# A hybrid S5/Hyena encoder layer in fp32: the input projections in another order

## Chip, core and metric

The kernel runs on one core of one Trainium2 chip. The metric is device time in microseconds (us); less is better. All data are fp32 in DRAM; the large products run in fp32r with a split into a high and a low part (three products per product).

## What is computed

One layer of a bidirectional encoder with x of 1024 tokens by 1024 channels:

```
xn = rmsnorm(x);  proj = xn @ w_in                      # 1024 x 7168
u_s5, g_s5, p_hy, g_hy, m_logits = split(proj)          # 512, 512, 3072, 1024, 2048
y_s5 = s5_mixer(u_s5, g_s5, ...) @ w_branch_s5          # scan both ways, GELU, GLU, * silu(g_s5)
v, x1, x2 = split(short_conv_3(p_hy))                   # centred, width 3
z = v
for o, g in enumerate((x1, x2)):                        # two long convolutions by FFT
    z = g * (irfft(rfft(z, 2L) * kf[o])[:L] + d[o] * z)
y_hy = (z * silu(g_hy)) @ w_branch_hy
m = sigmoid(m_logits)
out = rmsnorm(x + (m[:, :1024] * y_s5 + m[:, 1024:] * y_hy) @ w_out)
```

## The kernel before

**Projections.** A projection makes one block of 128 output channels for all 1024 tokens (`proj`, L528; `projs`, L532): 3 passes (high weight by high x, high by low x, low by high x) of 16 matmuls of 128x512 into a PSUM tile `pps` of which there are two, then a function `use` that empties it. The 56 column blocks of `w_in` are named by number here: 0 to 3 are u, 4 to 7 the S5 gate, 8 to 15 v, 16 to 23 x1, 24 to 31 x2, 32 to 39 the Hyena gate (SiLU), 40 to 55 the merge gates m (sigmoid). The products with `s5_w_glu` and `w_branch_s5` have half as many matmuls (24). Weights come through a short pipeline (`prefetch`, L501): a load on SP's queue into one of three `wraw` buffers, a cast on ScalarE (`whi`), a subtraction mostly on GpSimd (`wlo`), two buffers each. The list `self.order` (L492) gives the order of the weights, so the order of the projections is fixed.

**Emptying.** A gate block (`merge_gate`, L729) needs one ScalarE activation and a store to DRAM. A v, x1 or x2 block needs `conv` (L555): one ScalarE pass and two VectorE passes (L564, L566), then a fold of the time axis on VectorE and GpSimd (L782 and L783 for v, L585 to L587 for x1, L589 to L591 for x2). All of these pass through the two buffers `cv` of the pool `ev`.

**Stages.** After the filters come: the S5 scan, four blocks of channels (`s5_block`), bound up with VectorE's scans, with three merge gates beside each block; two v blocks and the last four merge gates; the S5 tail (`s5_tail`, L1259: reload the scan's result `d_y` as `ty`, split it into `tyh` and `tyl`, GLU products, one more v block, the branch products); the forward spectra of v (`hy_forward0`, L789: transposes `zt` of the folded v, DFT matmuls `fwe` and `fwo`, products with the filter spectra on VectorE, store to DRAM) with the other v blocks as they are needed; the first way back (`hy_inverse0`, L806: inverse DFT matmuls `iv`, times x1, transposed again); the second spectra (`hy_forward1`, L846), beside pairs of Hyena gate and x2 blocks; the second way back (`hy_inverse1`), branch product, merge, output product.

**Who sets the order.** A scheduler reorders the instructions of the program before it is compiled, by priorities and estimated times; on the chip each engine then runs its own list strictly in order, and waits at the head of it. Matmuls of projections are put among the DFT matmuls by that scheduler.

Of the kernel before, what the change touches and what calls it, by code (L numbers as in the profile page):

```python
# [9 lines left out]
F = mybir.dt.float32  # L10
# [7 lines left out]
L = 1024  # L18
# [82 lines left out]
class Trunk:  # L101
# [627 lines left out]
    def merge_gate(self):  # L729

        nc, c = self.nc, self.n_m
        if c == 16:
            return
        self.n_m += 1

        def use_m(ps):
            t = self.ev.tile([128, L], F, name="cv")
            nc.scalar.activation(out=t, in_=ps, func=AF.Sigmoid)
            nc.scalar.dma_start(out=self.d_m[c], in_=t)
        self.proj(40 + c, use_m)  # L740
# [31 lines left out]
    def hy_v(self):  # L772

        nc, c = self.nc, self.n_v
        if c == 8:
            return
        self.n_v += 1

        def use_v(ps):
            t = self.conv(ps, c, "cv")  # L780
            o = self.folded[c] = self.vp.tile([128, 2, 2, 2, 128], F, name="fv")
            nc.vector.tensor_tensor(out=o[:, 0], in0=self.plus(t), in1=self.minus(t), op=ALU.add)  # L782
            nc.gpsimd.tensor_tensor(out=o[:, 1], in0=self.plus(t), in1=self.minus(t), op=ALU.subtract)  # L783
            nc.vector.tensor_copy(out=o[:, 0, 0, 0, 0:1], in_=t[:, 512:513])
            nc.vector.tensor_scalar(out=o[:, 1, 0, 0, 0:1], in0=t[:, 0:1], scalar1=-1.0, scalar2=None, op0=ALU.mult)

        self.proj(8 + c, use_v)

    def hy_forward0(self):  # L789

        with ExitStack() as ctx:
            wp, fwd = self.fwd_pools(ctx, 0)
            for c in range(10):
                while self.n_v < min(8, c + 1):
                    self.hy_v()
                if c % 2 and c > 1:
                    next(f), next(f)
                if 0 < c < 9:
                    if c % 2:
                        z = wp.tile([128, 2, 2, 8, 128], R, name="z")  # L800
                    self.to_time(self.pf, self.folded.pop(c - 1).rearrange("p a b c d -> p (a b c d)"), z[:, (c - 1) % 2])
                if c % 2 == 0 and c:
                    f = fwd(c // 2 - 1, z)
                    next(f), next(f)

    def hy_inverse0(self):  # L806
# [3 lines left out]
        with ExitStack() as ctx:  # L810
# [3 lines left out]
            pt = ctx.enter_context(tc.tile_pool(name="iv_pt", bufs=2, space=PSUM, side="right"))  # L814
            gates, back = {}, {}
# [17 lines left out]
            for c in range(10):  # L833
# [7 lines left out]
                if 0 < c < 9:  # L841
                    rotate(c - 1)
                if c > 1:
                    store(c - 2)

    def hy_forward1(self, tail):  # L846

        nc = self.nc
        self.d_x2 = self.dram.tile([8, 128, L], F, name="d_x2")
        with self.tc.tile_pool(name="sg", bufs=1) as sp, self.tc.tile_pool(name="vf1", bufs=2) as self.vf, \  # L850
# [14 lines left out]
            for c in range(8):  # L865
                silu = sp.tile([128, L], F, name="sg")

                def use_g(ps):
                    nc.scalar.activation(out=silu, in_=ps, func=AF.Silu)

                def use_x2(ps):
                    t = self.vf.tile([128, 2, 2, 2, 128], F, name="vf")
                    self.fold(self.conv(ps, 16 + c, "cv"), silu, t)
                    nc.scalar.dma_start(out=self.d_x2[c], in_=t.rearrange("p a b c d -> p (a b c d)"))

                for i, (col, use) in enumerate(((32 + c, use_g), (24 + c, use_x2))):
                    self.proj(col, use)
                    for _ in range((2, 3, 0)[(2 * c + i) % 3]):
                        next(f, None)
                    if 2 * c + i == 11:  # L880
                        ctx.close()
                        tail()
# [191 lines left out]
    def s5_first(self, gb, p4, sp, ps_s):  # L1074
# [7 lines left out]
        self.merge_gate()  # L1082
# [33 lines left out]
    def s5_block(self, gb, p4, sp, ps_s):  # L1116
# [32 lines left out]
        self.merge_gate()  # L1149
# [77 lines left out]
        self.merge_gate()  # L1227
# [15 lines left out]
    def s5_inputs(self, c0, c1):  # L1243
        nc, d = self.nc, self.dram
        if c0 == 0:
# [4 lines left out]
            self.n_m = 0  # L1250
# [163 lines left out]
    def run(self):  # L1414
        tc = self.tc
        with ExitStack() as ctx:
# [28 lines left out]
            with ExitStack() as c4:  # L1445
                with tc.tile_pool(name="fv", bufs=3) as self.vp:
                    self.d_spec, self.folded, self.n_v = {}, {}, 0
                    with tc.tile_pool(name="vf0", bufs=2) as self.vf:
                        self.hy_v()
                        self.hy_v()  # L1450
                        while self.n_m < 16:
                            self.merge_gate()
                        self.s5_tail()
# [30 lines left out]
```

## Time and profile before

| | us |
|---|---|
| median of 3 runs | 1487.98 (1487.80 to 1488.49) |
| the profiled execution | 1488.18 |
| its span, first to last instruction | 1486.4 |
| TensorE busy in the span | 1358.1 (91%) |
| VectorE busy | 1100.0 (74%) |
| ScalarE, GpSimd busy | 447.0, 486.4 |

The profiled execution lies 0.2 us above the median, and 1.8 us of it lie outside the span. TensorE is busy nine tenths of the time, and the amount of its work does not depend on the order; so the table is read for where TensorE is not busy, and which engine it waits for there.

### The profile page before, as it was taken

Reading aid. Unit: us, or ns where it says so; the run is one execution under the profiler, and the core shown is the slowest. Engines: PE = TensorE matmul, PEld = TensorE weight load, DVE = VectorE, ACT = ScalarE, POOL = GpSimd, SP = SyncE. Lnnn points to the kernel's source line nnn. Section 1 sums busy time; section 2 is a strip of 40 time slices with the busy share of each in tenths; the row PEclk is TensorE's granted clock in tenths of the full one; section 3 lists DMA queues with packets and bytes.
Section 4 is the critical chain, followed back from the end, with each engine's and each line's share of the span. In section 5 each row is a group of like instructions: output and inputs, shape, how many; then the busy total and the mean of one; then the engine's idle time right before and its main releaser. Section 6 shows DMA issues by size and latency. Waiting matters only on the chain. (4 is left out here: it accounts for less than half of the span.)

```text
span 1486.4 us, 19375 instructions
## 1 busy us (share of the span) xinstructions
PE 1358.1 (91%) x7219; PEld 1143.8 (77%) x7219; DVE 1100.0 (74%) x1963; ACT 447.0 (30%) x661; POOL 486.4 (33%) x306
## 2 busy tenths in 40 slices
PE   5888999998988989899999998999999944999998
PEld 3767888786867868688888776888888844978886
DVE  7999996899789887525479998454569994943532
ACT  4666662122222122232121211333321112511322
POOL 3756764114111111234223312245412111333222
PEclk9998999999999999899999999999999976999999
DMA  8221224622652323243853345645477669633432
GB/s 270 86 71 72 106 86 158 170 86 71 216 160 77 86 74 74 78 143 116 276 182 114 128 140 188 191 158 167 156 267 265 219 209 314 205 131 112 127 111 75
DMA packets 177673, 220.52 MB, mean 148 GB/s; under 512 B 21853, under 2 KB 142937, under 8 KB 174844
## 3 DMA queue, kind: packets, MB, share of 16 engines
q1 hardware_dynamic: 149212, 153.69, 33.8%
q10 hardware_dynamic: 27792, 62.45, 11.6%
q0 software_dynamic: 576, 3.15, 0.6%
q8 instruction: 57, 0.93, 0.3%
q14 instruction: 36, 0.29, 0.1%
HBM read 147.49 MB, written 76.82 MB: 151 GB/s over the span
## 5 line engine op out<-in xcount | busy, mean ns | idle before, releaser
L513 POOL TENSOR_TENSOR wlo<-wraw,whi 128x1024 fp32r<-128x1024 f32 (+1 forms) x67 | 169.6, 2533 | 588.1 <-PE pps L542 412.4
L542 PE MATMUL pps<-xh,whi 128*128 128x512 f32 x896 | 234.4, 408 | 11.5 <-DVE cv L566 11.5
L542 PE MATMUL pps<-xh,wlo 128*128 128x512 f32 x896 | 228.1, 401 | 0.0
L542 PE MATMUL pps<-xl,whi 128*128 128x512 f32 x896 | 226.0, 399 | 0.0
L542 PEld LDWEIGHTS pps<-xh,whi 128*128 128x128 f32 x896 | 169.9, 194 | 50.1 <-issue 12.3
L542 PEld LDWEIGHTS pps<-xh,wlo 128*128 128x128 f32 x896 | 169.2, 191 | 38.9
L542 PEld LDWEIGHTS pps<-xl,whi 128*128 128x128 f32 x896 | 167.9, 190 | 38.9 <-issue 0.2
L510 ACT CAST whi<-wraw 128x1024 fp32r<-128x1024 f32 (+1 forms) x76 | 74.7, 984 | 348.3 <-PE pps L542 276.1
L404 PE MATMUL po<-sh,fo 128*128 128x256 f32 x512 | 101.4, 292 | 6.0 <-DVE sh L111 5.1
L635 PEld LDWEIGHTS iv<-ic,y 128*128 128x128 f32 x752 | 96.5, 193 | 4.8 <-DVE y L113 2.3
L113 DVE TENSOR_TENSOR y<-yraw,y 128x512 fp32r<-128x512 f32 x64 | 61.7, 979 | 51.5 <-ACT y L109 51.2
L635 PE MATMUL iv<-ic,y 128*128 128x256 f32 (+1 forms) x752 | 98.4, 286 | 1.5 <-DVE y L113 1.5
L404 PEld LDWEIGHTS po<-sh,fo 128*128 128x128 f32 x512 | 84.3, 197 | 8.2 <-DVE sh L111 6.1
L357 POOL TENSOR_TENSOR acc<-acc,sq 128x512 f32<-128x512 f32 x56 | 76.3, 1362 | 25.0 <-ACT sq L342 22.8
L404 PE MATMUL po<-sl,fo 128*128 128x256 f32 x256 | 74.4, 291 | 1.0 <-DVE sl L113 1.0
L109 ACT CAST y<-yraw 128x512 fp32r<-128x512 f32 x64 | 39.3, 620 | 92.3 <-PE iv L635 54.1
L722 DVE TENSOR_TENSOR m<-m 128x512 f32<-128x512 f32 x64 | 53.0, 848 | 0.0
L404 PEld LDWEIGHTS po<-sl,fo 128*128 128x128 f32 x256 | 50.5, 197 | 2.3 <-DVE sl L113 1.5
L686 PE MATMUL fwo<-z,zc 128*128 128x256 f32 x384 | 50.1, 283 | 0.5 <-DVE x L716 0.5
L333 PE MATMUL g<-w3h,ha 128*128 128x512 f32 x64 | 33.0, 516 | 19.1 <-DVE e L338 17.3
L686 PEld LDWEIGHTS fwo<-z,zc 128*128 128x128 f32 x384 | 48.5, 191 | 1.6 <-DVE x L716 0.7
L336 ACT ACTIVATE e<-dec,negt 128x512 f32<-128x512 f32 x64 | 45.2, 716 | 10.6 <-DVE so L350 4.8
(437 smaller groups left out, 2685.1 us busy)
## 6 DMA issues: line engine op xcount, KB each, us to landing
wraw<-w_in SPq DMA_DIRECT2D x56, 512.0 KB, 4.6
kspec<-ko SPq DMA_DIRECT2D x32, 512.0 KB, 3.0
kt<-kspec SPq DMA_DIRECT2D x32, 512.0 KB, 3.3
d_y<-x ACTq DMA_DIRECT2D x32, 512.0 KB, 6.0
yraw<-d_y SPq DMA_DIRECT2D x64, 256.0 KB, 4.8
d_m<-cv ACTq DMA_DIRECT2D x16, 512.0 KB, 2.9
d_z<-z ACTq DMA_DIRECT2D x8, 1024.0 KB, 9.8
z<-d_z SPq DMA_DIRECT2D x8, 1024.0 KB, 10.9
```

The source lines that it names most:

```text
L109: nc.scalar.copy(out=hi, in_=src)
L113: e.tensor_tensor(out=lo, in0=src, in1=hi, op=ALU.subtract)
L333: nc.tensor.matmul(out=ps, lhsT=ha[:, tsl], rhs=w3h, start=True, stop=False)
L336: nc.scalar.activation(out=e, in_=decf, func=AF.Exp, scale=negt[:, tt:tt + 1])
L357: nc.gpsimd.tensor_tensor(out=acc, in0=acc, in1=sq, op=ALU.add)
L404: nc.tensor.matmul(out=po[:, part], lhsT=fo[a][:, 12 * (jj % 2) + b], rhs=sd[4 + i][d][:, part], start=n == 0 and part == 0, stop=n == 11 ...
L510: nc.scalar.copy(out=hi, in_=raw)
L513: eng.tensor_tensor(out=lo, in0=raw, in1=hi, op=ALU.subtract)
L542: nc.tensor.matmul(out=ps[:, hf * 512:hf * 512 + 512], lhsT=w[:, kc], rhs=part(x, kc, hf), start=a == 0 and p == 0 and kc == 0, stop=b == ...
L635: nc.tensor.matmul(out=dst, lhsT=lhsT, rhs=self.ic[b][:, j, cols], start=first, stop=last)
L686: nc.tensor.matmul(out=out, lhsT=zc[a][:, b], rhs=z[:, :, d, zi], start=start and n == 0, stop=stop and n == 3 * len(prods) - 1)
L722: nc.vector.tensor_tensor(out=m[:, part, :, 0], in0=m[:, part, :, 0], in1=m[:, part, :, 1], op=op)
```

## The change

The gate blocks (merge and Hyena gate, 24 "pure" blocks, ScalarE alone) become one list and can stand anywhere; the Hyena gates go to DRAM (`d_sg`) and are loaded again when their x2 block is folded. The S5 blocks take twelve pure blocks as before. The four merge gates that stood behind the scan are gone from there. All eight v blocks are made in and right behind the S5 tail, stored to DRAM (`d_v`) and loaded again for the transposes. Six pure blocks stand beside the forward spectra. The first way back has its eight x1 blocks and four x2 blocks, the second spectra six pure blocks and the other four x2 blocks, of which the last two are written behind the spectra.

```
-        self.order = i(range(0, 8), range(40, 52), range(8, 10), range(52, 56))
+        self.pure = [*range(40, 48), *range(32, 40), *range(48, 56)]
+        self.order = i(range(0, 8), self.pure[:12], range(8, 10))
         self.order += [("s5_w_glu", c, 4) for c in range(4)] + i(range(10, 11))
-        self.order += [("w_branch_s5", c, 4) for c in range(8)] + i(range(11, 24))
-        self.order += i(*((32 + c, 24 + c) for c in range(8)))
+        self.order += [("w_branch_s5", c, 4) for c in range(8)] + i(range(11, 16), self.pure[12:18])
+        self.order += i(*((16 + c,) + ((24 + c // 2,) if c % 2 else ()) for c in range(8)))
+        self.order += i(self.pure[18:20], (28,), self.pure[20:22], (29,), self.pure[22:24], (30, 31))
...
+    def gate_columns(self):
+        nc, col = self.nc, self.pure.pop(0)
+        func, out = (AF.Sigmoid, self.d_m[col - 40]) if col >= 40 else (AF.Silu, self.d_sg[col - 32])
+        def use(ps):
+            t = self.ev.tile([128, L], F, name="cv")
+            nc.scalar.activation(out=t, in_=ps, func=func)
+            nc.scalar.dma_start(out=out, in_=t)
+        self.proj(col, use)
+
+    def hy_x2(self, c, sp, vp):
+        nc = self.nc
+        def use_x2(ps):
+            silu = sp.tile([128, L], F, name="sg")
+            nc.sync.dma_start(out=silu, in_=self.d_sg[c])
+            t = vp.tile([128, 2, 2, 2, 128], F, name="vf")
+            self.fold(self.conv(ps, 16 + c, "cv"), silu, t)
+            nc.scalar.dma_start(out=self.d_x2[c], in_=t.rearrange("p a b c d -> p (a b c d)"))
+        self.proj(24 + c, use_x2)
...
         def use_v(ps):
             t = self.conv(ps, c, "cv")
-            o = self.folded[c] = self.vp.tile([128, 2, 2, 2, 128], F, name="fv")
+            o = self.vp.tile([128, 2, 2, 2, 128], F, name="fv")
...
+            nc.scalar.dma_start(out=self.d_v[c], in_=o.rearrange("p a b c d -> p (a b c d)"))
...
             for c in range(10):
-                while self.n_v < min(8, c + 1):
+                while self.n_v < 8:
                     self.hy_v()
+                if c < 8:
+                    folded[c] = self.vp.tile([128, L], F, name="fv")
+                    self.nc.sync.dma_start(out=folded[c], in_=self.d_v[c])
+                if c > 1 and len(self.pure) > 6:
+                    self.gate_columns()
...
                 if 0 < c < 9:
                     rotate(c - 1)
+                if c < 8 and c % 2:
+                    self.hy_x2(c // 2, sp, sp)
...
-            for c in range(8):
...
-                for i, (col, use) in enumerate(((32 + c, use_g), (24 + c, use_x2))):
-                    self.proj(col, use)
-                    for _ in range((2, 3, 0)[(2 * c + i) % 3]):
+            for i in range(10):
+                if i == 8:
+                    for _ in f:
+                        pass
+                    ctx.close()
+                    tail()
+                if i < 8 and i % 3 < 2:
+                    self.gate_columns()
+                else:
+                    self.hy_x2((4, 5, 6, 7)[i // 3 if i < 8 else i - 6], sp, self.vf)
+                if i < 8:
+                    for _ in range(2 if i % 2 else 3):
                         next(f, None)
...
                         self.hy_v()
                         self.hy_v()
-                        while self.n_m < 16:
-                            self.merge_gate()
                         self.s5_tail()
```

How the engines' lists change, at three places. TensorE at the end of the S5 scan (`s5ps` are the last products of the scan, `sr` and `si` its VectorE results; `pps` with `xh`, `xl` is a projection from x, with `tyh`, `tyl` one from the scan's reloaded result). Before:

```order
1365 L542 MATMUL pps<-xl,whi 128x512 x16
1366 L542 MATMUL pps<-xh,wlo 128x512 x16
1367 L542 MATMUL pps<-xh,whi 128x512 x16
1368 L542 MATMUL pps<-xl,whi 128x512 x5
1369 L1236 MATMUL s5ps<-sr,pr 128x128 x2
1370 L542 MATMUL pps<-xl,whi 128x512 x11
```

Between row 1390, the last product of the scan, and row 1401, the first with `tyh`, the list before holds the rest of this projection and three more from x. Now:

```order
1365 L544 MATMUL pps<-xl,whi 128x512 x16
1366 L544 MATMUL pps<-xh,wlo 128x512 x16
1367 L1253 MATMUL s5ps<-sr,pr 128x128 x2
1368 L1254 MATMUL s5ps<-si,pi 128x128
```

and the scan's last product is followed at once by the products with the reloaded result:

```order
1386 L1254 MATMUL s5ps<-si,pi 128x128
1387 L544 MATMUL pps<-tyh,whi 128x512 x14
1388 L544 MATMUL pps<-tyl,whi 128x512 x6
1389 L544 MATMUL pps<-tyh,whi 128x512 x2
1390 L544 MATMUL pps<-tyl,whi 128x512 x8
1391 L544 MATMUL pps<-tyh,wlo 128x512 x8
```

ScalarE's list at the same place (`y` is the GELU of the scan's products, `d_v` the new store of a folded v, `d_g` the S5 gate, `ty` the reload). Now:

```order
321 L1255 ACT_TABLE_LOAD
322 L1255 ACTIVATE y<-s5ps 128x512 x2
323 L798 DMA d_v<-fv 128x1024
324 L1294 DMA cv<-d_g 128x1024
325 L798 DMA d_v<-fv 128x1024
326 L1294 DMA cv<-d_g 128x1024
327 L1285 DMA ty<-d_y 128x1024 x4
328 L1286 CAST tyh<-ty 128x1024 x4
```

Before, one sigmoid, its table load and its store stood between `y` and the reload; now two stores of v and two gate loads do.

VectorE's list where the second spectra begin (`ke` is their first product; L564 and L566, now L566 and L568, are the two passes of `conv`, L590 and L591, now L592 and L593, the fold of an x2 block). Before:

```order
1480 L564 SCALAR_TENSOR_TENSOR cv<-pps,cw,cv 128x1023
1482 L566 SCALAR_TENSOR_TENSOR cv<-pps,cw,cv 128x1023
1484 L590 TENSOR_TENSOR vf<-cv,sg 128x512
1485 L591 TENSOR_TENSOR vf<-cv,sg 128x1
1486 L513 TENSOR_TENSOR wlo<-wraw,whi 128x1024
1487 L704 TENSOR_TENSOR ke<-fwe,eo_9003 128x512
```

Now:

```order
1487 L515 TENSOR_TENSOR wlo<-wraw,whi 128x1024
1488 L566 SCALAR_TENSOR_TENSOR cv<-pps,cw,cv 128x1023
1489 L568 SCALAR_TENSOR_TENSOR cv<-pps,cw,cv 128x1023
1490 L592 TENSOR_TENSOR vf<-cv,sg 128x512
1491 L593 TENSOR_TENSOR vf<-cv,sg 128x1
1492 L706 TENSOR_TENSOR ke<-fwe,eo_9414 128x512
```

The block folded here is the fourth x2 block before and the fifth now; from `ke` to the end of the spectra the list held four more before (rows 1487 to 1640) and holds three now (rows 1492 to 1640). On TensorE the number of projection matmuls ahead of the first DFT matmul of the second spectra, over the whole program, is 11 higher than before.

## Rows read from the trace of the kernel before

**Rows 1.** The page: span, and TensorE's line of part 1.

```profile
span 1486.4 us, 19375 instructions
PE 1358.1 (91%) x7219; PEld 1143.8 (77%) x7219; DVE 1100.0 (74%) x1963; ACT 447.0 (30%) x661; POOL 486.4 (33%) x306
```

**Rows 2.** Waits of TensorE: us in total, times, longest.

```profile
PE iv L633 <- DMA yraw<-d_y: 40.3, 1, 40.3
PE s5ps L1236 <- DVE sr L1223: 17.1, 3, 6.6
PE pps L542 <- DVE cv L566: 11.5, 2, 7.2
```

**Rows 3.** Windows by stage: us, busy PE, PEld, DVE, ACT, POOL, clock, DMA, GB/s.

```profile
735.00:746.00 11.00, 11.00 (x49) 8.86 (x48) 5.11 (x6) 3.18 (x6) 2.43 (x1) 1.00 1.02 364
746.00:884.00 138.00, 133.92 (x740) 113.94 (x739) 130.62 (x165) 29.11 (x36) 37.63 (x13) 0.99 0.39 132
884.00:936.80 52.80, 48.43 (x202) 38.63 (x201) 42.59 (x48) 10.17 (x10) 10.21 (x4) 0.97 0.63 209
936.80:1092.00 155.20, 155.20 (x885) 134.66 (x884) 79.52 (x125) 51.90 (x74) 66.65 (x35) 1.00 0.54 176
1092.00:1207.30 115.30, 115.08 (x647) 99.70 (x645) 106.13 (x136) 19.44 (x22) 15.83 (x6) 1.00 0.68 232
1207.30:1247.80 40.50, 0.23 (x2) 0.02 (x1) 26.87 (x31) 2.87 (x3) 8.83 (x2) 0.53 0.81 273
```

**Rows 4.** Timeline of TensorE, end of the scan: start, us, what, idle before.

```profile
591.95 3.90 PE L542 MATMUL pps<-xh,wlo 128*128 128x512 f32 x16
603.01 6.62 PE L542 MATMUL pps<-xh,whi 128*128 128x512 f32 x16 [7.17 <-DVE cv L566]
...
613.88 0.38 PE L1237 MATMUL s5ps<-si,pi 128*128 128x128 f32 x2
...
618.26 3.76 PE L542 MATMUL pps<-xh,wlo 128*128 128x512 f32 x15
...
651.72 3.90 PE L542 MATMUL pps<-xh,wlo 128*128 128x512 f32 x16
655.46 2.02 PE L542 MATMUL pps<-tyh,whi 128*128 128x512 f32 x8
```

**Rows 5.** Timeline of VectorE at the same place.

```profile
606.37 1.22 DVE L1226 TENSOR_TENSOR si<-si,f 128x1024 f32<-128x1024 f32 x1
...
618.10 4.11 DVE L782 TENSOR_TENSOR fv<-cv 128x512 f32<-128x512 f32 x2 [9.32 <-PE s5ps L1235]
...
635.37 3.82 DVE L1269 TENSOR_TENSOR tyl<-ty,tyh 128x1024 fp32r<-128x1024 f32 x2 [0.67 <-ACT tyh L1268]
```

**Rows 6.** Timeline of ScalarE at the same place.

```profile
618.54 0.60 ACT L1238 ACTIVATE y<-s5ps 128x512 f32<-128x512 f32 x1 [1.64 <-PE s5ps L1237]
...
625.50 2.09 ACTq L1267 DMA_DIRECT2D ty<-d_y  x4
631.07 1.05 ACT L1268 CAST tyh<-ty 128x1024 fp32r<-128x1024 f32 x1 [6.20 <-DMA ty<-d_y]
...
636.16 1.03 ACT L1268 CAST tyh<-ty 128x1024 fp32r<-128x1024 f32 x1
```

**Rows 7.** Timeline of GpSimd at the same place.

```profile
618.14 6.08 POOL L783 TENSOR_TENSOR fv<-cv 128x512 f32<-128x512 f32 x2 [19.82 <-PE s5ps L1235]
```

**Rows 8.** Timeline of TensorE behind the first spectra.

```profile
901.84 5.52 PE L542 MATMUL pps<-xh,whi 128*128 128x512 f32 x16 [4.37 <-DVE cv L566]
```

**Rows 9.** VectorE by line, 950 to 1250 us: busy, mean ns.

```profile
L590 DVE TENSOR_TENSOR vf<-cv,sg 128x512 f32<-128x512 f32 x8 | 14.9, 1865 | 0.0
L564 DVE SCALAR_TENSOR_TENSOR cv<-pps,cw,cv 128x1023 f32<-128x1023 f32 x9 | 11.5, 1280 | 7.7 <-ACT cv L563 7.7
...
L591 DVE TENSOR_TENSOR vf<-cv,sg 128x1 f32<-128x1 f32 x8 | 5.0, 628 | 0.1
```

**Rows 10.** Timeline of VectorE, end of the second spectra.

```profile
1233.55 0.69 DVE L725 TENSOR_TENSOR x<-m 128x512 f32<-128x512 f32 x1
```

More of the change, by code (lines that the diff above doesn't have):

```diff
@@ L792, in hy_forward0 @@
             wp, fwd = self.fwd_pools(ctx, 0)
+            folded = {}
             for c in range(10):
-                while self.n_v < min(8, c + 1):
+                while self.n_v < 8:
                     self.hy_v()
+                if c < 8:
[3 more added lines that the diff above has]
+                    self.gate_columns()
                 if c % 2 and c > 1:
@@ L800, in hy_forward0 @@
                         z = wp.tile([128, 2, 2, 8, 128], R, name="z")
-                    self.to_time(self.pf, self.folded.pop(c - 1).rearrange("p a b c d -> p (a b c d)"), z[:, (c - 1) % 2])
+                    self.to_time(self.pf, folded.pop(c - 1), z[:, (c - 1) % 2])
                 if c % 2 == 0 and c:
@@ L814, in hy_inverse0 @@
             pt = ctx.enter_context(tc.tile_pool(name="iv_pt", bufs=2, space=PSUM, side="right"))
+            sp = ctx.enter_context(tc.tile_pool(name="iv_x2", bufs=1, side="right"))
+            self.d_x2 = self.dram.tile([8, 128, L], F, name="d_x2")
             gates, back = {}, {}
@@ L848, in hy_forward1 @@
         nc = self.nc
-        self.d_x2 = self.dram.tile([8, 128, L], F, name="d_x2")
         with self.tc.tile_pool(name="sg", bufs=1) as sp, self.tc.tile_pool(name="vf1", bufs=2) as self.vf, \
@@ L864, in hy_forward1 @@
             next(f)
-            for c in range(8):
[L866 to L874, printed above, removed]
-                for i, (col, use) in enumerate(((32 + c, use_g), (24 + c, use_x2))):
-                    self.proj(col, use)
-                    for _ in range((2, 3, 0)[(2 * c + i) % 3]):
+            for i in range(10):
[10 more added lines that the diff above has]
+                    for _ in range(2 if i % 2 else 3):
                         next(f, None)
-                    if 2 * c + i == 11:
-                        ctx.close()
-                        tail()
     def exp(self, pool, out, x, shape):
@@ L1081, in s5_first @@
                               in_=self.d_u[gb].rearrange("(g h) (t k) -> t h g k", h=16, t=8)[t])
-        self.merge_gate()
+        self.gate_columns()
         new = lambda n, tag: p4.tile([128, 1024], F, name=n, tag=tag, bufs=S5B[tag])
@@ L1148, in s5_block @@
                     V.tensor_copy(out=dst[bw, :, 1], in_=src[bw])
-        self.merge_gate()
+        self.gate_columns()
         cni = sp.tile([128, 128], F, name="cni", tag="cni")
@@ L1226, in s5_block @@
         V.tensor_tensor(out=si, in0=si, in1=f0, op=ALU.add)
-        self.merge_gate()
+        self.gate_columns()
         y = new("y")
@@ L1249, in s5_inputs @@
             self.d_m = d.tile([16, 128, L], F, name="d_m")
-            self.n_m = 0
+            self.d_sg = d.tile([8, 128, L], F, name="d_sg")
+            self.d_v = d.tile([8, 128, L], F, name="d_v")
         for c in range(c0, c1):
@@ L1446, in run @@
                 with tc.tile_pool(name="fv", bufs=3) as self.vp:
-                    self.d_spec, self.folded, self.n_v = {}, {}, 0
+                    self.d_spec, self.n_v = {}, 0
                     with tc.tile_pool(name="vf0", bufs=2) as self.vf:
@@ L1450, in run @@
                         self.hy_v()
-                        while self.n_m < 16:
-                            self.merge_gate()
                         self.s5_tail()
```

9 lines of the change are left out of this document (removed).

## Prediction, made before the changed kernel ran

> **What bounds the kernel now.** I read the page first: TensorE is busy 1358.1 of 1486.4 us [rows 1]. The change adds no matmul, so its worth is in the 128 us in which TensorE stands. The list of TensorE's waits says where [rows 2]: one of 40.3 us for the first `yraw` of the second way back, 17.1 us for `sr` of the scan and 11.5 us for the VectorE pass of `conv` that frees a PSUM tile. The windows by stage [rows 3] give the rest: beside the first spectra (746 to 884) TensorE is busy 133.9 of 138.0 us while VectorE is busy 130.6, and from 884 to 936.8 it loses another 4.4; in the first way back it loses nothing (155.2 of 155.2) and VectorE is only half busy; beside the second spectra it loses 0.2 of 115.3; then come the 40.5 us in which it does 0.2 us of work. The last view is the timeline at the end of the scan, engine by engine [rows 4 to 7]. There the reader is to see that TensorE works from 603 on without a gap while the scan's result is stored, reloaded and split: that work is the four merge gates which the change takes away.
>
> **Sum, against the profiled execution's own 1488.2 us** (0.2 above the median of the three runs). A difference under 3 us (0.2%) cannot be told from none.
>
> *A projection's price.* A run of 16 matmuls starts 3.74 us before the next [rows 4], a projection has three: 11.2 us. Four are 44.8 us. They are not saved, they stand in later stages where TensorE is full [rows 3], so time won ahead of them must reach 44.8 us to break even.
>
> *The end of the scan: +25 us.* Before, the first product with `tyh` starts at 655.46. For the changed kernel I follow the chain. The second v block ends at 591.95 + 3.90 = 595.85 [rows 4]. Nothing but the scan's own products follows in TensorE's list, and they need `si`, ready at 606.37 + 1.22 = 607.6 [rows 5]. From the first `si` product to the last they took 618.26 - 613.88 = 4.4 us [rows 4], but at full clock. After a stand of 7.17 us 16 matmuls took 6.62 us where others take 3.90 [rows 4], so a stand costs about 2.7 us more; here the stand is over 8 us. The scan then ends at T = 607.6 + 4.4 + 2.7 = 614.7, against 618.3 before.
> From T on, before: the reload `ty` is issued at 625.50 = T + 7.2, the first cast starts at 631.07 = T + 12.8 and the last ends at 637.2 = T + 18.9 [rows 6]; the last low half ends at 639.2 [rows 5]. In the changed kernel the reload stands on ScalarE's queue behind two stores of v, and the second needs GpSimd's fold, which ends at 618.14 + 6.08 = T + 5.9 [rows 7]. So the issue is again near T + 7, whatever ScalarE saves by the sigmoid that is gone. New is the traffic: two stores of v and two gate loads, 512 KB each, of which one of each is issued right ahead of the reload. At the 364 GB/s that the DMA engines moved when they were full [rows 3], 1.05 MB are 2.9 us. So casts begin near T + 15.7, four follow one another at 1.05 us [rows 6], and the last ends at T + 19.9. The list lets 14 high-part matmuls start before a low part is needed; 6 of them (1.4 us) lie behind that cast's first need, so TensorE starts as if without a gap at T + 18.5 = 633.2, and another 2.7 us for the clock make 635.9. That is 19.6 us earlier than 655.46, with 44.8 us less done: **+25.2**. Bounds: no loss by the clock and no traffic in the way, +17; all 2.1 MB ahead of the reload (5.8 instead of 2.9 us) and folds slowed as well, +30.
>
> The Trainium skill (page "Trainium Kernel Development and Optimization", section Key Constraints) says that transfers issued from the SP, ACT and POOL queues all run on the same 16 DMA engines and interleave. By that rule the v stores do delay the reload, as taken here; were the queues independent, the gap would be +22 and the sum 1502. No row of this trace has v stores beside the reload.
>
> *The v blocks and their trip through DRAM: 0.* Per v the VectorE and GpSimd work stays, only earlier, between 655 and the spectra, one per 11.2 us of TensorE; two passes of 1.28 [rows 9], a fold of some 2 us and GpSimd's 3.0 [rows 7] fit. The eight stores go through ScalarE's queue, the eight loads through SP's, where the first stand behind six weight loads and so come only once the last v block's matmuls are over and a weight is split (cast 1.05, subtraction at most 2.4); with 5 us for the load that is 9 us, covered by the gate projection (11.2 us) which stands between. If that cover is short, up to 5 us are lost, once. The DMA engines are 0.39 busy there [rows 3].
>
> *The gates beside the spectra and `d_sg`: 0.* ScalarE is busy 29.1 of 138 us there [rows 3] and has to do a v's pass anyway; eight stores on its queue and eight loads on SP's are added. Where the fold of the first x2 block has to wait for the memory of the first spectra it keeps one of two `cv` buffers; the other serves the x1 blocks, bound 0 to 5 us.
>
> *The first spectra: -6 us.* The losses before are 4.1 us (746 to 884) and 4.4 us (884 to 936.8) [rows 3], and the run of 16 after that wait took 5.52 instead of 3.90 [rows 8]: 10.1 together. VectorE was busy 173.2 us in this stretch against TensorE's 182.3, ratio 0.95. Between the first DFT matmul and the first inverse one the changed lists have 501 projection matmuls instead of 578 (10.4 projections instead of 12.0), 18 us less for TensorE, and six blocks with `conv` instead of twelve on VectorE, at about 4.2 us (two passes of 1.28, fold and ends some 1.6) 25 us less: 148 against 164, ratio 0.90. VectorE gains room, but not much; I take 6 of the 10 back. Bounds: all 10; or -4 (a loss), since TensorE's list runs DFT matmuls in longer pieces, and each waits for VectorE to free the PSUM tiles.
>
> *The second spectra and the wait of 40.3 us: -2.4 us.* This is where the largest wait is, and little of it goes. VectorE is busy 106.1 of 115.3 us beside the spectra and ends them at 1234.2 [rows 3, 10], 26.9 us after the projections ran out at 1207.3; the remaining 13.5 us are the reload of the inverse constants. Its work here is nearly the same: the gates never touched VectorE, and from the first `ke` to the end three x2 blocks stand instead of four. One is two passes of 1.28 and a fold of 1.87 + 0.63 [rows 9], 5.0 us. Against that, 11 more projection matmuls (2.6 us) stand ahead of the spectra. So -5.0 + 2.6; bounds -6 and +3.
>
> Sum: 1488.2 + 25.2 - 6 - 2.4 = **1505 us**.
>
> **Rivals.**
> *The first spectra give nothing back* (chance 0.20). For it: the longer pieces of DFT matmuls, and that the stretch was bound by VectorE to 95% and will be to 90%. Against: twelve blocks with `conv` become six. With 0 instead of -6 it is 1511, with the loss of 4 it is 1515.
> *The gap is short* (0.13). If the clock costs nothing in the scan's few products and the reload lands as it did, the term is +17: 1497. For it: T and the reload's times are rows; the traffic is an assumption. Against: the loss by the clock stands in rows 4 and 8 both.
> *Faster: the wait before the second way back goes* (0.04). It is VectorE that is late there, by 26.9 us. Were all four x2 blocks out of the way of the second spectra (written behind them, the last two are), 20 us would go, with the 10.1 of the first spectra all gone and no other matmuls ahead; 1488.2 + 25.2 - 10.1 - 20 is 1483. It decides from about 19 us won there, with 6 in the first spectra. VectorE's list shows three of the four still inside, so this needs the chip to be limited by something else than that list.
> *The change does not do what it says* (0.02): if TensorE found other work at the end of the scan the sum would be 1488.2 - 8.4 = 1480, or 1488 without the gains. The list leaves no such work, since TensorE runs in order.
>
> **How the numbers follow.** The forecast's own case has 0.61: 1505. The range takes the short gap on one side and most of the first rival on the other: 1494 to 1516. Faster by over 0.2% (below 1485): the third and half of the fourth rival, 0.05. Within 0.2%: a short gap with every gain at its bound (1488.2 + 17 - 10 - 6 = 1489), 0.04. Slower: 0.91.
>
> **What would show it.** In the changed profile TensorE's waits should have a new one of over 15 us ahead of the first product with `tyh`, released by the cast or the low half, with a granted clock near the lower of its two levels (1.2 GHz) in that stretch, as in the 40.5 us before (0.53, [rows 3]); the first matmul with `tyh` should start near 633 (within 4 us). The waits of 746 to 937 should shrink to a few us at a place some 12 us later. The wait for `yraw` should be 35 to 41 us. Wrong would be a start with `tyh` before 625, or a wait before the second way back under 25 us, or new losses over 10 us in the first way back, where I have put none.

## The result, and the profile after

The changed kernel took 1511.72 us (median of 4 runs, 1510.84 to 1513.64), the kernel before on the same chip 1488.24 (1487.80 to 1489.76): ratio 1.0158, 95% interval 1.0140 to 1.0175. It is slower by 23.5 us, and the forecast was 1505 with a range of 1494 to 1516. The profiled execution took 1512.0 us.

The page of the changed kernel, span and engines, answers to [rows 1]:

```profile
span 1510.2 us, 19464 instructions
...
PE 1354.7 (90%) x7219; PEld 1141.0 (76%) x7219; DVE 1108.0 (73%) x1963; ACT 449.9 (30%) x663; POOL 489.5 (32%) x306
```

TensorE has the same 7219 matmuls. It stands for 155.5 us now (1510.2 - 1354.7) and stood for 128.3 before. TensorE's waits, as in [rows 2]:

```profile
PE iv L635 <- ACT y L109: 49.5, 2, 47.7
PE s5ps L1253 <- DVE sr L1240: 23.3, 4, 6.6
PE pps L544 <- ACT tyh L1286: 19.1, 1, 19.1
```

The third is new: it is the gap behind the scan. The first, ahead of the second way back, was 40.3 and is 47.7. The windows by stage (columns as in [rows 3]) are the gap, first spectra, first way back, second spectra, and the stand behind them:

```profile
610.80:629.80 19.00, 0.00 (x0) 0.00 (x0) 3.96 (x6) 1.62 (x2) 6.28 (x3) 0.60 0.70 201
...
786.88:949.82 162.94, 160.06 (x862) 136.01 (x860) 146.47 (x179) 34.15 (x42) 26.34 (x10) 1.00 0.57 191
949.82:1111.20 161.38, 158.68 (x895) 136.84 (x896) 87.77 (x136) 53.65 (x75) 67.10 (x35) 1.00 0.61 200
1111.20:1225.00 113.80, 112.85 (x635) 97.54 (x633) 107.15 (x128) 18.38 (x21) 18.67 (x6) 1.00 0.69 244
1225.00:1272.80 47.80, 0.09 (x1) 0.00 (x1) 31.79 (x37) 2.87 (x3) 9.21 (x3) 0.54 0.80 276
```

The ends of the last four windows are events: the first DFT matmul of the first spectra, the first inverse one, the first DFT matmul of the second spectra, the last projection, and the first inverse one of the second way back. One more place is common to both kernels, the first matmul of the third v block. By these places the 23.8 us between the two spans divide without a rest:

| place or piece, us | before | after | difference | forecast |
|---|---|---|---|---|
| start of the third v block | 678.0 | 655.3 | -22.7, with 44.8 less done: gap +22.1 | +25.2 |
| start of the first way back | 936.8 | 949.8 | +13.0, less the gap: first spectra -9.1 | -6 |
| first way back, length | 155.3 | 161.4 | +6.1 | +2.6 |
| second spectra and the wait behind them | 155.7 | 161.6 | +5.9 | -5.0 |
| second way back to the end | 238.6 | 237.4 | -1.2 | 0 |

### The profile page after: what moved, and what is told of

It reads as the page before. It is cut to its first block, busy times and chain, and to the rows that moved or that the text cites. A ratio compares the mean times of both kernels' runs of the same rounds, so it can differ in the third digit from the quotient of the medians.

```text
span 1510.2 us, 19464 instructions
## 1 busy us (share of the span) xinstructions
PE 1354.7 (90%) x7219; PEld 1141.0 (76%) x7219; DVE 1108.0 (73%) x1963; ACT 449.9 (30%) x663; POOL 489.5 (32%) x306
## 5 line engine op out<-in xcount | busy, mean ns | idle before, releaser
L544 PE MATMUL pps<-xh,whi 128*128 128x512 f32 x896 | 230.2, 402 | 0.9 <-DVE cv L568 0.9
L544 PE MATMUL pps<-xh,wlo 128*128 128x512 f32 x896 | 223.7, 398 | 0.0
L113 DVE TENSOR_TENSOR y<-yraw,y 128x512 fp32r<-128x512 f32 x64 | 58.0, 923 | 44.1 <-ACT y L109 43.9
L357 POOL TENSOR_TENSOR acc<-acc,sq 128x512 f32<-128x512 f32 x56 | 76.0, 1357 | 22.9 <-ACT sq L342 22.1
L566 DVE SCALAR_TENSOR_TENSOR cv<-pps,cw,cv 128x1023 f32<-128x1023 f32 x24 | 30.7, 1279 | 38.6 <-ACT cv L565 38.5
L724 DVE TENSOR_TENSOR m<-m 128x512 f32<-128x512 f32 x64 | 51.8, 836 | 0.0
L565 ACT ACTIVATE cv<-pps,cb,cw 128x1024 f32<-128x1024 f32 x24 | 29.0, 1207 | 76.5 <-PE pps L544 41.2
L591 POOL TENSOR_TENSOR vf<-cv,sg 128x512 f32<-128x512 f32 x8 | 27.9, 3493 | 72.6 <-DVE cv L568 36.0
L635 PE MATMUL iv<-icp,y 128*128 128x512 f32 x16 | 6.8, 427 | 49.5 <-ACT y L109 49.5
```

Of the source, the lines that this page charges most:

```text
L113: e.tensor_tensor(out=lo, in0=src, in1=hi, op=ALU.subtract)
L357: nc.gpsimd.tensor_tensor(out=acc, in0=acc, in1=sq, op=ALU.add)
L544: nc.tensor.matmul(out=ps[:, hf * 512:hf * 512 + 512], lhsT=w[:, kc], rhs=part(x, kc, hf), start=a == 0 and p == 0 and kc == 0, stop=b == ...
L565: nc.scalar.activation(out=t, in_=ps, func=AF.Identity, scale=w[1], bias=self.cb[:, c:c + 1])
L566: nc.vector.scalar_tensor_tensor(out=t[:, 1:], in0=ps[:, 0:L - 1], scalar=w[0], in1=t[:, 1:], op0=ALU.mult, op1=ALU.add)
L724: nc.vector.tensor_tensor(out=m[:, part, :, 0], in0=m[:, part, :, 0], in1=m[:, part, :, 1], op=op)
```

## The end of the scan in the changed kernel

Timeline of TensorE (columns as in [rows 4]): the scan's last products, the first with `tyh`, and the third v block.

```profile
610.39 0.39 PE L1254 MATMUL s5ps<-si,pi 128*128 128x128 f32 x2
629.88 5.86 PE L544 MATMUL pps<-tyh,whi 128*128 128x512 f32 x14 [19.10 <-ACT tyh L1286]
...
655.33 3.90 PE L544 MATMUL pps<-xh,whi 128*128 128x512 f32 x16
```

SP's queue at the same place, with the duration of the issue:

```profile
611.43 6.89 SPq L1257 DMA_DIRECT2D d_y<-y  x8
```

ScalarE and its queue at the same place:

```profile
614.64 0.33 ACTq L798 DMA_DIRECT2D d_v<-fv  x1
615.00 0.46 ACTq L1294 DMA_DIRECT2D cv<-d_g  x1
616.54 0.33 ACTq L798 DMA_DIRECT2D d_v<-fv  x1
616.96 0.45 ACTq L1294 DMA_DIRECT2D cv<-d_g  x1
625.13 1.77 ACTq L1285 DMA_DIRECT2D ty<-d_y  x4
628.78 1.04 ACT L1286 CAST tyh<-ty 128x1024 fp32r<-128x1024 f32 x1 [17.37 <-DMA ty<-d_y]
```

The last of the eight issues alone, and the longest wait of SP's queue between two of them:

```profile
618.02 0.30 SPq L1257 DMA_DIRECT2D d_y<-y  x1
...
SPq L1257 <- DMA d_v<-fv: 3.3, 1, 3.3
```

The scan ends at T = 610.8 (610.39 + 0.39). The reload `ty` is issued at T + 14.3, where it was T + 7.2 before [rows 6]. It needs the eight small stores of `d_y`, and these were late for two reasons. Seven were issued by 614.7, but the eighth waited 3.3 us, which the profile puts down to a store of `d_v` that had to land first (in the trace both signal the same semaphore, which would explain it; no run tests that). Then 7.1 us passed from its issue at 618.02 to that of the reload, beside the 2.1 MB of `d_v` and `d_g`. The first cast starts at T + 18.0, and TensorE follows it at once.

## VectorE in the second spectra

VectorE by line, 1095 to 1250 us of the kernel before (busy, mean ns, idle before):

```profile
L722 DVE TENSOR_TENSOR m<-m 128x512 f32<-128x512 f32 x32 | 24.1, 780 | 0.0
...
L725 DVE TENSOR_TENSOR x<-m 128x512 f32<-128x512 f32 x16 | 12.9, 808 | 0.0
...
L715 DVE TENSOR_TENSOR x<-ke,fwo 128x512 f32<-128x512 f32 x16 | 10.9, 680 | 1.9 <-DMA d_y<-x 1.9
```

The same three lines of the changed kernel, 1112 to 1275 us:

```profile
L724 DVE TENSOR_TENSOR m<-m 128x512 f32<-128x512 f32 x32 | 25.4, 820 | 0.0
...
L727 DVE TENSOR_TENSOR x<-m 128x512 f32<-128x512 f32 x16 | 17.2, 1076 | 0.0
...
L717 DVE TENSOR_TENSOR x<-ke,fwo 128x512 f32<-128x512 f32 x16 | 10.9, 680 | 4.3 <-DMA d_y<-x 4.3
```

The 16 instructions of one line took 4.3 us more, and the timelines show which of them: some that met a GpSimd operation. VectorE's timeline of the changed kernel, from two places and the end of the list:

```profile
1192.10 0.68 DVE L726 TENSOR_TENSOR x<-m 128x512 f32<-128x512 f32 x1
1192.70 2.90 DVE L727 TENSOR_TENSOR x<-m 128x512 f32<-128x512 f32 x1
...
1248.55 0.69 DVE L726 TENSOR_TENSOR x<-m 128x512 f32<-128x512 f32 x1
1249.16 2.83 DVE L727 TENSOR_TENSOR x<-m 128x512 f32<-128x512 f32 x1
...
1256.23 0.68 DVE L727 TENSOR_TENSOR x<-m 128x512 f32<-128x512 f32 x1
```

GpSimd's timeline at those two places:

```profile
1192.54 2.51 POOL L515 TENSOR_TENSOR wlo<-wraw,whi 128x1024 fp32r<-128x1024 f32 x1 [22.68 <-PE pps L544]
...
1248.90 2.53 POOL L515 TENSOR_TENSOR wlo<-wraw,whi 128x1024 fp32r<-128x1024 f32 x1 [6.40 <-ACT whi L512]
```

An operation of 0.68 us took 2.90 and 2.83 us while GpSimd split a weight beside it, and ended 0.6 us after GpSimd did. Over the whole list from the first `ke` to the last `x`, seven entries of VectorE's timeline (one operation, or two alike in a row) are more than 0.3 us longer than the shortest of their line would make them. All seven overlap a GpSimd operation, and together they are 14.7 us too long; some 15 others that overlap one take their usual time. In the kernel before there are six such entries, all beside GpSimd, with 8.4 us. VectorE's list from the first `ke` to the last `x` took 139.8 us (1117.1 to 1256.9) against 135.5 before (1098.73 to 1234.24), with one x2 block fewer in it.

## Experiments

Each kernel was timed beside the kernel before on one chip; ratios are to that, with 95% intervals. The changed kernel itself stands at 1.0158.

### Cover at the end of the scan

```
-        self.order = i(range(0, 8), self.pure[:12], range(8, 10))
+        self.order = i(range(0, 8), self.pure[:12], range(8, 14))
-        self.order += [("s5_w_glu", c, 4) for c in range(4)] + i(range(10, 11))
+        self.order += [("s5_w_glu", c, 4) for c in range(4)] + i(range(14, 15))
...
-                        self.hy_v()
-                        self.hy_v()
+                        for _ in range(6):
+                            self.hy_v()
                         self.s5_tail()
```

> The changed kernel with v blocks 2 to 5 made ahead of the S5 tail, so that four projections from x stand again between the scan's last products and the first product with tyh; all else as in the changed kernel. Theory (the 22 us lost there are missing cover and nothing else): the wait of 19.1 us ahead of tyh goes, and the time falls by 18 to 22 us, to about 1491 (1488 to 1495). Rival (a v block is a poor cover, since its passes on VectorE and its fold on GpSimd stand in the way of the split into tyh and tyl, and its store in the way of the reload): 8 us or more of the wait stay, 1500 or above.

1488.51 us, ratio 0.9994 (0.9985 to 1.0004): 23 us back, and the time of the kernel before. The wait ahead of `tyh` is gone; its first product starts at 654.47 behind four full projections, where it stood at 655.46 in [rows 4]. v blocks cover the reload as well as gates did. The 22 us were missing cover: in the profiled execution 23.2 us come back in the gap. (Another 4.1 are lost again before the first spectra, and 5.5 come back in the spectra.)

### The gates back behind the scan

```
-        self.order = i(range(0, 8), self.pure[:12], range(8, 10))
+        self.order = i(range(0, 8), self.pure[:12], range(8, 10), self.pure[12:16])
...
+                        for _ in range(4):
+                            self.gate_columns()
                         self.s5_tail()
```

> The changed kernel with four gate blocks put back behind the scan, so that two instead of six are left beside the first spectra. Theory (the gap is missing cover; the first spectra need TensorE 160 of 163 us but VectorE 146 of them, so that work taken out of them shortens them only down to VectorE's time): the gap's 22 us come back, 45 us of work go in there, and the first spectra get 12 to 16 us shorter, not 45: 1512 - 22 + 45 - 14, about 1521 (1516 to 1526), so slower than the changed kernel. Rival (the first spectra shrink by all that is taken out): about 1490.

1534.12 us, ratio 1.0302 (1.0286 to 1.0317): 13 us worse than the theory's own figure and outside its range. The gap closed (`tyh` at 657.3), but the first spectra did not get shorter at all: 167.5 us instead of 162.9. Their window:

```profile
812.20:979.70 167.50, 138.38 (x767) 118.03 (x765) 147.62 (x181) 29.27 (x37) 26.00 (x9) 0.93 0.52 174
```

TensorE's timeline at their end:

```profile
979.72 0.79 PE L635 MATMUL iv<-icp,y 128*128 128x512 f32 x1 [26.88 <-ACT y L109]
```

VectorE is as busy as ever (147.6 us), and TensorE stands for 26.9 us ahead of the first way back, until the first `yraw` has been reloaded and split. So the first spectra last as long as VectorE's list and a reload behind it. The four gates had cost nothing beside them; put back behind the scan they cost 44.8 us less the gap's 22, and 22.4 us were measured. That these agree so well is luck: the first spectra took 4.6 us more with four gates fewer, and the second spectra 7.1 us less (154.5) with the same blocks.

### The reload first

```
-            nc.scalar.dma_start(out=self.d_v[c], in_=o.rearrange("p a b c d -> p (a b c d)"))
+            if c < 2:
+                self.late.append((self.d_v[c], o.rearrange("p a b c d -> p (a b c d)")))
+            else:
+                nc.scalar.dma_start(out=self.d_v[c], in_=o.rearrange("p a b c d -> p (a b c d)"))
...
+            with tc.issue_after(ld.ins):
+                for out, o in self.late:
+                    nc.scalar.dma_start(out=out, in_=o)
...
+                    with tc.issue_after(ld.ins):
+                        nc.scalar.dma_start(out=g, in_=self.d_g[c])
```

(`ld` is the last load of `ty`.)

> The changed kernel with the two stores of v and the S5 gate loads issued behind the four loads of ty on ScalarE's queue instead of ahead of them; no other order is changed. Theory (of the 22 us, about 7 are the stores and gate loads, which slow the small stores of d_y and so the reload): the store of d_y takes some 3.7 us again instead of 6.9, the reload is issued 7 us earlier, near 618 instead of 625, the wait of 19.1 us shrinks to 11 to 13, and the time falls by 6 to 8 us, to about 1505. Rival (the whole 22 us are missing cover, the transfers cost nothing): the same time within 2 us, 1510 to 1514.

1505.68 us, ratio 1.0119 (1.0102 to 1.0135): 6 us back, as the theory had it. SP's queue at the end of the scan:

```profile
611.85 3.67 SPq L1260 DMA_DIRECT2D d_y<-y  x8
```

ScalarE's queue, the reload:

```profile
617.48 1.77 ACTq L1288 DMA_DIRECT2D ty<-d_y  x4
```

The same eight stores are issued in 3.67 us instead of 6.89, the reload 2.4 us after the last of them (615.09) instead of 7.1, 7.6 us earlier in all, and TensorE's wait is 11.1 instead of 19.1 us.

### Two x2 blocks behind the second spectra

```
-            self.fold(self.conv(ps, 16 + c, "cv"), silu, t)
+            with ExitStack() as late:
+                if c > 5:
+                    late.enter_context(self.tc.issue_after(self.last_x.ins))
+                self.fold(self.conv(ps, 16 + c, "cv"), silu, t)
```

(`last_x` is the last VectorE product of the second spectra.)

> The changed kernel with the VectorE part (conv and fold) of the last two x2 blocks held behind the last product of the second spectra; their matmuls stay where the scheduler puts them. Theory (the second spectra last as long as VectorE's list does, and TensorE has nothing to do for 47.7 us behind its last projection): VectorE's list up to the last x is shorter by two blocks, 10 us, and some 2 to 4 more by GpSimd's folds that no longer run beside it; the two blocks then run in the 16 us in which the constants of the second way back load, and the time falls by 10 to 14 us, to about 1500 (1497 to 1503). Rival (the wait is set by transfers, or the two blocks now delay the split of yraw by as much): 1510 to 1514.

1502.94 us, ratio 1.0099 (1.0084 to 1.0114): 9 us back, a little less than the 10 to 14 expected. VectorE's timeline behind the last product:

```profile
1242.89 0.68 DVE L727 TENSOR_TENSOR x<-m 128x512 f32<-128x512 f32 x1
1243.49 2.46 DVE L566 SCALAR_TENSOR_TENSOR cv<-pps,cw,cv 128x1023 f32<-128x1023 f32 x2
...
1259.06 1.43 DVE L113 TENSOR_TENSOR y<-yraw,y 128x512 fp32r<-128x512 f32 x2 [8.53 <-ACT y L109]
```

The last `x` ends at 1243.6 instead of 1256.9, TensorE starts the second way back 13.7 us earlier, at 1259.1, and 3.6 us come back there (241.0 instead of 237.4), where the second block's fold stands among the splits. The second spectra are VectorE's.

### GpSimd's half of the fold taken away

```
-            G.tensor_tensor(out=o[:, 0], in0=self.plus(t), in1=self.plus(g), op=ALU.mult)
+            if part:
+                self.nc.scalar.copy(out=o[:, 0], in_=self.plus(t))
+            else:
+                G.tensor_tensor(out=o[:, 0], in0=self.plus(t), in1=self.plus(g), op=ALU.mult)
...
-            self.fold(self.conv(ps, 16 + c, "cv"), silu, t)
+            self.fold(self.conv(ps, 16 + c, "cv"), silu, t, c > 3)
```

(The last argument is `part`. This kernel leaves out the product with the Hyena gate in that half.)

> The changed kernel, with the GpSimd half of the fold of x2 blocks 4 to 7 given to ScalarE as a plain copy; the product with the Hyena gate is left out in that half. Theory (VectorE's instructions take two to four times as long while GpSimd runs a fold beside them, some 8 to 10 us in the second spectra): VectorE's list from the first ke to the last x takes 4 to 7 us less than the 139.8 us of the changed kernel, and the time falls by as much, to 1505 to 1508. Rival (the slow VectorE instructions have another cause, or the halves only move the collisions to the weight splits): within 2 us of the changed kernel, 1510 to 1514.

1509.52 us, ratio 1.0140 (1.0127 to 1.0154), which can't be told from the changed kernel's and lies between the two ranges. In the stage itself the theory's figure is there: from `ke` at 1119.27 to the last `x` at 1254.0 VectorE took 134.7 us, 5.1 less, and the stretch from the first DFT matmul to the second way back 157.2 instead of 161.6. That alone would prove little, since versions with the same blocks in this stage differ by as much. But with the same 160 instructions VectorE was busy 125.8 instead of 135.0 us in its list, and the entries that are too long fell from seven with 14.7 us to three with 5.3, all beside weight splits. VectorE stood 4.0 us longer in its list, which took back part of that. The expected 4 us are not seen in the total; the second spectra began 1.9 us later in this execution. VectorE's list still meets weight splits. VectorE's timeline near the end of the list:

```profile
1247.05 3.25 DVE L724 TENSOR_TENSOR m<-x,kt 128x1024 f32<-128x1024 f32 x1
1250.22 1.21 DVE L725 TENSOR_TENSOR m<-x,kt 128x1024 f32<-128x1024 f32 x1
```

GpSimd's at the same place:

```profile
1246.57 2.65 POOL L515 TENSOR_TENSOR wlo<-wraw,whi 128x1024 fp32r<-128x1024 f32 x1 [49.36 <-ACT whi L512]
```

### The gates alone, in the kernel before

```
-        self.order = i(range(0, 8), range(40, 52), range(8, 10), range(52, 56))
+        self.order = i(range(0, 8), range(40, 52), range(8, 10))
...
-        self.order += [("w_branch_s5", c, 4) for c in range(8)] + i(range(11, 24))
+        self.order += [("w_branch_s5", c, 4) for c in range(8)] + i((52, 11, 53, 12, 54, 13, 55, 14, 15), range(16, 24))
...
+                if 1 < c < 6:
+                    self.merge_gate()
...
-                        while self.n_m < 16:
-                            self.merge_gate()
```

> The kernel before with one part of the change alone: the four merge gates that stood behind the scan stand beside the first spectra (with the v blocks 3 to 5); v stays in SBUF, x1, x2 and the Hyena gates stay where they were. Theory (the gap's price depends on the traffic of v beside the reload; without it, as in the run with the reload first, the first product with tyh starts near 622 against 655.5): 33 us earlier there, for 44.8 us less done, so +11 to +12; in the first spectra TensorE is already busy 182 of 191 us, so the four projections lengthen them by 37 to 45 us: together 4 to 12 us more than before, 1493 to 1501. Rival 1 (the gap costs 22 us without v's stores too): tyh near 630 and 1503 to 1511. Rival 2 (VectorE sets the first spectra, the gates fit beside it): they grow by less than 25 us, and the time is 1485 or below.

1484.12 us, ratio 0.9971 (0.9960 to 0.9982): 4 us faster than the kernel before, where 4 to 12 us slower was expected, and rival 2 by its numbers, though VectorE does not set these spectra: TensorE is busy 202.6 of 204.3 us there. `tyh` starts at 627.55, so by this place the gap's price is 44.8 - 27.9 = 16.9 us (19.2 in the changed kernel); by the start of the third v block, as in the table, it is 19.7 us (22.1 in the changed kernel). The windows of first spectra, first way back and second spectra:

```profile
720.30:924.60 204.30, 202.56 (x1044) 170.23 (x1043) 163.03 (x207) 42.41 (x49) 55.54 (x20) 1.00 0.47 156
924.60:1083.30 158.70, 158.68 (x898) 137.41 (x899) 80.36 (x126) 53.76 (x75) 66.44 (x34) 1.00 0.53 177
1083.30:1246.00 162.70, 131.92 (x718) 112.86 (x716) 141.80 (x170) 24.72 (x28) 28.78 (x9) 0.92 0.69 232
```

The first spectra grew by 13.6 us, not 37: TensorE does 20 us more there (202.6 against 182.4 [rows 3]) and its idle time falls from 8.4 to 1.7. The other 25 us or so of the 44.8 were handed on: the x1 blocks that the gates displaced went into the first way back (158.7 against 155.2 busy), the blocks that those displaced into the second spectra (131.9 against 115.1 + 0.2), where they fill part of what was the longest wait: 29.4 us instead of 40.3. These two stretches got 10.3 us longer for it.

### The two edits together, and two more versions

Cover by v blocks and late x2, both edits as above on the changed kernel:

> The changed kernel with both of the edits that helped: v blocks 2 to 5 ahead of the S5 tail, and the VectorE part of the last two x2 blocks behind the second spectra. Theory (two places, each with its own bound): the gains add, 23 and 9 us, to about 1479.5 (1477 to 1483), 0.6% below the kernel before. Rival (in the first of the two runs the wait ahead of the second way back was already 2 us shorter, and part of the late gain has gone with it): 1483 to 1487.

1480.01 us, ratio 0.9947 (0.9934 to 0.9959): the gains add, and it beats the kernel before by 0.5%.

The gates alone with the late x2 (the `with` of the fourth experiment around the fold in `use_x2` of the kernel before):

> The kernel of the run with the gates alone (1484.1), with the VectorE part of the last two x2 blocks behind the second spectra, as in the run with x2 late. Theory (the second spectra last as long as VectorE's list in every version, and the wait ahead of the second way back, 29.4 us here, is what that list outlasts TensorE's work by): VectorE's list gets two blocks shorter, 10 us, of which some 3 come back in the second way back, as there: 1475 to 1478. Rival (that wait is 11 us shorter here than in the kernel before, so TensorE or the reload of the constants is nearly as late as VectorE): 1481 to 1485.

1481.65 us, ratio 0.9955 (0.9938 to 0.9971), the rival's number, by a new wait (TensorE's list of waits):

```profile
PE pps L542 <- DVE cv L566: 20.3, 2, 20.0
```

The first of the two late blocks holds one of the two `pps` tiles, and in this order the projection of the second late block is still to be made: it waits 20.0 us for that tile, until the first block's `conv` behind the last `x`, and then takes 13 us ahead of the second way back (its first 16 matmuls 5.58 us, where others take 3.90). The second spectra get 6.8 us shorter (155.9 instead of 162.7), and 3.5 come back in the second way back.

Cover and late x2, and two gates moved from the first to the second spectra:

```
-        self.order += [("w_branch_s5", c, 4) for c in range(8)] + i(range(15, 16), self.pure[12:18])
+        self.order += [("w_branch_s5", c, 4) for c in range(8)] + i(range(15, 16), self.pure[12:16])
...
-        self.order += i(self.pure[18:20], (28,), self.pure[20:22], (29,), self.pure[22:24], (30, 31))
+        self.order += i(self.pure[16:18], (28,), self.pure[18:20], (29,), self.pure[20:24], (30, 31))
...
-                if c > 1 and len(self.pure) > 6:
+                if c > 1 and len(self.pure) > 8:
...
-            for i in range(10):
-                if i == 8:
+            for i in range(12):
+                if i == 10:
...
-                if i < 8 and i % 3 < 2:
+                if i in (0, 1, 3, 4, 6, 7, 8, 9):
...
-                    self.hy_x2((4, 5, 6, 7)[i // 3 if i < 8 else i - 6], sp, self.vf)
+                    self.hy_x2({2: 4, 5: 5}.get(i, i - 4), sp, self.vf)
```

> The kernel with cover and late x2 (1480.0), with two of its six gate blocks moved from the first spectra to the second ones; by the program's list TensorE then has 1.1 projections (12 us) fewer ahead of the second spectra and as many more in them. Theory (the first spectra are as long as VectorE makes them, as in the run with the gates back, so the two gates' place is taken there by x1 blocks; the first way back is bound by TensorE and gets 12 us shorter, and the 35 us wait ahead of the second way back takes the work): 8 to 12 us less, 1468 to 1472. Rival 1 (the x1 blocks lengthen VectorE's list in the first spectra by 4 to 8 us, which eats most of it): 1474 to 1479. Rival 2 (the first way back is not bound by TensorE but by its own chain, and does not get shorter): 1480 or above.

1478.96 us, ratio 0.9933 (0.9918 to 0.9948), not to be told from the 0.9947 of the version without it, and at the upper end of rival 1's range. The first way back got 6.3 us shorter (154.5), half of the 12. Its window:

```profile
933.41:1087.95 154.54, 150.13 (x837) 131.00 (x838) 83.47 (x135) 52.33 (x74) 64.99 (x35) 0.96 0.62 203
```

TensorE has 8.1 us less to do there than without the edit (158.2), but stands for 4.4 of the 154.5 us instead of 2.7. The first spectra took 3.2 us more (rival 1), and the execution stood 2.8 us later already at the first product with `tyh`, ahead of anything this edit moves; why is not known. The wait ahead of the second way back is down to 23.5 us.

## Why the prediction was right, and where it was not

**The sign and the main term held.** The gap was put at +25.2 and is +22.1; the run with cover shows that it is missing cover, since the whole of it goes with four other blocks there. Its parts compensate. The scan ended earlier than estimated (T = 610.8, not 614.7): the estimate took 7.1 us from `si` to the end, it was 6.3, and `si` itself was ready 3 us earlier. The reload was issued at T + 14.3, not T + 7, and there the step failed that put it "again near T + 7" and added 2.9 us for 1.05 MB of traffic: the traffic acts ahead of the reload's issue, through the small stores of `d_y` on which the reload waits. TensorE then started on the first cast instead of as if behind the last; its slow start is real (granted clock 0.60 in the gap, near the lower of its two levels, 1.2 GHz). That the term comes within 3 us of the measured one is therefore partly luck.

**The traffic ahead of the reload.** From the scan's end to the issue of the reload the runs show 6.3 us with nothing in the way (617.48 - 611.19, reload first), 9.0 with 1 MB of gate loads (622.65 - 613.66, gates alone) and 14.3 with 2.1 MB (changed kernel). In the run with the gates alone the eight stores were issued as fast as with nothing in the way (3.68 us), so its 2.7 us are traffic beside them. The Trainium skill (page "Trainium Kernel Development and Optimization", section Key Constraints) has transfers of the SP, ACT and POOL queues on the same 16 DMA engines, interleaving. These 2.7 us agree with it. Of the 8 us in the changed kernel 3.3 are the wait of the eighth store, the other 4.7 lie between its issue and the reload's; the prediction put 2.9 on all of it. The 7.2 us of the kernel before are no measure of traffic, since its reload stood on ScalarE's queue behind a sigmoid that ended at 624.9:

```profile
623.85 1.03 ACT L738 ACTIVATE cv<-pps 128x1024 f32<-128x1024 f32 x1
```

**First spectra: -9.1 against -6,** inside its bounds. The run with the gates back shows what the working missed: there is a floor of VectorE's list and the reload behind it, 167.5 us there with 138 us of work for TensorE, against 162.9 here with 160. The six gates fill that floor almost exactly: TensorE stands for 2.9 us in the first spectra, where it stood for 8.4. Some 4 of the 9.1 us are no gain, but work that went over the border into the first way back, where TensorE does 3.5 us more.

**Second spectra: forecast -2.4 with the first way back, measured +12.0.** This is the step that failed: "its work here is nearly the same ... three x2 blocks stand instead of four ... 5.0 us". The list did lose a block (15.2 us of conv and fold instead of 18.2, so 3.0 and not 5.0), but lines L724 and L727 took 5.6 us more, from meeting GpSimd's splits and folds, and the waits for the stores of `x` 2.4 us more. So VectorE needed 139.8 us instead of 135.5, and the reload behind it 15.9 instead of 13.5. GpSimd's share is shown by the run without its half of the fold, in the stage, not in the total. How much of the 4.3 us belongs to the order itself is open. VectorE's list took 138.7 us in the run with the reload first, where it is the same operation for operation, and 136.5 (cover) and 132.9 (gates back) with the same blocks but some operations in another order. The entries that are too long make up 12.0, 11.7 and 8.0 us there instead of 14.7, so small shifts change where the two engines meet. The longer reload does recur: 15.5 to 16.4 us in every version of the changed kernel. Why the stores and the reload landed later was not tried. The first way back was forecast at +2.6 and cost 6.1: 3.5 us of matmuls and 2.7 us of stands, 2.5 of them one wait for `y`.

**The sum.** It missed by 7 us. The gap (3.1), the first spectra (3.1) and the stage from the second way back on (1.2) came out better than forecast, the first way back and the second spectra worse by 14.4. That 1505 is no further from 1512 is partly luck.

**The rivals.** "The first spectra give nothing" gave the nearest time, 1511, by the wrong mechanism: the first spectra gave more than the forecast, the second took it back. The price of the faster rival was right in kind: with two x2 blocks out of VectorE's way TensorE starts the second way back 13.7 us earlier.

**Its signs.** The wait over 15 us ahead of `tyh` (19.1), its start near 633 within 4 us (629.9) and the low clock are there; the wait for `yraw`, put at 35 to 41 us, is 47.7.

## What to carry to other kernels

Filler for a full engine is worth something only in a stretch where that engine stands, and there up to the stretch's floor. Gates, which need no VectorE, belong behind a reload or beside a stage that VectorE bounds; blocks with VectorE work belong where TensorE is the bound, or behind VectorE's last product. Before moving a block, follow what it displaces to the end of the program: moving the four gates alone gained 4 us, although the gap cost 17 to 20, since 25 us of the displaced work ended up where it cost 10. The whole change lost 23.5: it opened the same gap, gave TensorE no more work in the second spectra than before (112.9 us against 115.3), and the wait behind them grew.

## What was not expected of the hardware

- A VectorE operation of 0.68 us took 2.8 to 2.9 us, and one of 1.2 us 3.25, beside a GpSimd operation of about 2.5 us, and others beside such operations took no longer than usual. From the first `ke` to the last `x` of the second spectra no VectorE operation was over 0.3 us too long without GpSimd beside it, in this kernel and in the one before. A VectorE-bound stage pays for GpSimd's work at such places, 8 to 15 us here, and the sum changes with small shifts.
- Eight stores of 64 KB were issued in 6.89 us beside 2.1 MB of large transfers, in 3.67 without them; the difference is one wait of 3.3 us of the last store. The reload that needs them was issued 7.1 us after that store instead of 2.4: what waits for the small ones waits for the large.
